# First layer of a fused transformer kernel: split float32r products against plain float32 products, and GpSimd's arithmetic moved to VectorE

## The chip, the cores and the metric

The kernel runs on one core of one Trainium2 chip. A core has the engines TensorE (PE; its weight loads are PEld), VectorE (DVE), ScalarE (ACT), GpSimd (POOL) and SyncE (SP), which here only issues DMAs. The metric is device time in microseconds (us) of one execution; smaller is better.

## The reference, cut to what matters

A sequence of 256 tokens of width 1024 goes through two transformer layers and then through a further block with experts. Only the first layer's mixing part ("even" layer) is touched. It computes, in float32:

```
hn = rmsnorm(x);  q, k, v, u = split(hn @ even_w_in)          # 1024 -> 512+128+128+512
o_attn = local attention with sinks (8 query heads, 2 key heads, window 128)
lam = exp(dt * a);  h_t = lam * h_{t-1} + (w*b) u_t            # complex state, 32 groups x 64
y = Re(c h) + d*u;  y = gelu(y);  o_ssm = y * sigmoid(y @ w_glu + b_glu)
x = x + concat(o_attn, o_ssm) @ even_w_out                     # 1024 -> 1024
```

What follows (a feed-forward part, an attention layer, another feed-forward part, a mixer with two kinds of attention, a memory layer, 32 experts) is not touched.

## The kernel before, in words

The program is written as Python that emits instructions into tiles. A list scheduler decides each engine's order at build time, from dependencies, program order and a model of costs; `after(...)` adds an order by hand on one engine. Each engine then runs its own list in order.

A **split product** stores a float32 matrix as two float32r tiles: `put_split` (L181, L182) lets ScalarE write the rounded high part (`Copy`) and VectorE, or GpSimd where `self.low` says so, write the low part by a subtraction. `mm3` then makes three matmuls, high by high, high by low and low by high. All products with weights in the kernel are of this kind. A plain float32 product is one `matmul` in the code; the trace shows it as two PE records.

`even()` runs in this order of the program:

- `x` and the first weights are loaded. `Norm.part` turns x by 16 transposes; VectorE multiplies by the gain (L1714) and the halves are split (`exh`, `exl`).
- The product for u: 4 outputs of 128 rows by 8 slices of 128, 256 columns each (`gemm_ws`). Then q, k, v: 3 pieces of 256 columns by 2 halves of the tokens by 8 slices (`gemm_ts`). Each piece of weights of 1 MB is loaded by SP into one of three buffers (`wrot`), then split into `hrot`.
- `S5.scalars` computes the state-space factors, some 90 small VectorE instructions (powers by `cmul`, L1841 to L1843). `inputs` (L1926, L1938) writes the input factors into `bd`, `rotations` (L1966 to L1970) builds a table by doubling. `outputs` (L2010, L2012, L2017, L2022) computes the output factors Q on GpSimd.
- `inputs_T` transposes bd (PE group s5F), `direct` multiplies bd by Q (PE group s5K), ScalarE copies the result to KT in pieces of 32 partitions, and GpSimd adds the diagonal (L2045).
- `qk_norm` and `swa`: two blocks of attention; scores (sc), a masked maximum on VectorE (L616), exponentials on ScalarE, the transposed weights (pTp), the product with v (swo), then a split into `mixa`.
- `step(j)`, four times: VectorE turns the inputs by the table, runs the recurrence as a scan (L2084) and turns back; PE makes y from KT, Q and the states.
- `gate`: gelu, a reshuffle (yt), a split, the product with `ssm_w_glu` (glu: 4 outputs by 4 slices, 256 columns), sigmoid, product, a split into `mixb`.
- `out_proj`: 8 slices by 2 halves of the tokens by 2 halves of the columns, 512 columns each (acc); the half on `mixa` can run before `gate` is done. GpSimd makes the low parts of four slices of `even_w_out` and of `ssm_w_glu`.

Buffers: `wrot` has 3 and `hrot` 4 buffers of 8 KB per partition; the pool `rot` (`r8`) has 4 more for u, the two bd, tables, attention, steps and the gate.

Of the kernel before, what the change touches and what calls it, by code (L numbers as in the profile page):

```python
# [44 lines left out]
class K:  # L45
# [269 lines left out]
    def accumulate(self, acc, pieces, t, first, last, cs=(0, 1)):  # L315

        ts = slice(t * P, (t + 1) * P)
        k = [(lhs[f], wp[f]) for lhs, wp in pieces for f in range(len(lhs))]
        for c in cs:
            cols = slice(c * 512, (c + 1) * 512)  # L320
            for i, ((lh, ll), (wh, wl)) in enumerate(k):
                self.mm3(acc[t][c], (lh[:, ts], ll[:, ts]), (wh[:, 0, cols], wl[:, 0, cols]),
                         first and i == 0, last and i == len(k) - 1)
# [43 lines left out]
    def even(self, x):  # L367
        nc, a = self.nc, self.a
        ctx = ExitStack()
# [8 lines left out]
        ectx = ExitStack()  # L378
        s5.ff = self.pool("s5F", 1, ectx, side="right")
# [18 lines left out]
        gotten = nc.vector.tensor_copy(gc, pg[:, 0:8]).ins  # L398
# [3 lines left out]
        nrm = Norm(self, x, None, "ex")  # L402
        nrm.gc = gc, s5.work().rearrange("p (k n) -> p k n", k=8)
        xp = nrm.xp
        tw, order = [], []
        for c in range(2):
            with self.after(*order):
                for t in range(2):
                    nrm.part(t, c)
            if c == 0:  # L410
                with self.after(*self.hold):
                    tw.append(self.split(tu[0][:, :, 0:P]))
                order = self.last
        sub = self.hold[1]
        with self.after(order[1]):
            s5.scalars()
        with self.after(self.turned):
            self.warm(warm, 6)
        for j, t in enumerate(tu):
            for f in range(1 - j, 2):  # L420
                self.low = nc.gpsimd if len(tw) == 1 else None
                tw.append(self.split(t[:, :, f * P:(f + 1) * P]))
        self.hold = []
        after = self.last[0]
        uT = self.r8("uT")[:, 0:1024].rearrange("p (t b a) -> p t b a", t=4, b=4)
        pu = [self.ps("u") for _ in range(2)]
        for j in range(2):
            for f in range(2):
                self.gemm_ws(pu[j][:, f * S:(f + 1) * S], tw[2 * j + f], xp)
            if j == 0:  # L430
                with self.after(self.lastmm, self.last[0]):
                    s5.factors()

        qk = ep.tile([P, 2, 10, 64], F32)
        v = ep.tile([P, 2, P], F32)
        pq = []
        for j in range(3):
            pq.append(self.ps("qkv"))
            self.gemm_ts(pq[j], self.wcolk(w, j * 256), xp)
            if j == 0:  # L440
                with self.after(sub):
                    r, R = nrm.both()
                for i in range(2):
                    for f in range(2):
                        nc.vector.tensor_tensor(uT[:, 2 * i + f],
                                                pu[i][:, f * S:(f + 1) * S].rearrange("p (a b) -> p b a", b=4),
                                                R.rearrange("p (a b) -> p b a", b=4), op=OP.mult)
            pv = pq[j].rearrange("p (t h d) -> p t h d", t=2, d=64)
            for t in range(2):
                if j < 2:  # L450
                    nc.scalar.activation(qk[:, t, 4 * j:4 * j + 4], pv[:, t], AF.Copy, scale=r[:, t:t + 1])
                else:
                    nc.scalar.activation(qk[:, t, 8:10], pv[:, t, 0:2], AF.Copy, scale=r[:, t:t + 1])
                    nc.scalar.activation(v[:, t], pq[j][:, t * 256 + P:t * 256 + 256], AF.Copy, scale=r[:, t:t + 1])

        qg = ep.tile([P, 2, 2, 64], F32)
        for i, n in enumerate(("q_norm", "k_norm")):
# [4 lines left out]
        nc.sync.dma_start(bglu, a["ssm_b_glu"][0].rearrange("(t p) -> p t", p=P))  # L462
        s5.outputs()
        s5.inputs(after)
        sink8 = ep.tile([P, 8], F32)
        nc.vector.tensor_scalar(sink8.rearrange("p (g h) -> p g h", g=2),
                                sink.rearrange("p (h g) -> p g h", g=2), 8.0, None, op0=OP.mult)
# [3 lines left out]
        nc.gpsimd.tensor_tensor(qg[:, 0], qg[:, 0], qg[:, 1], op=OP.mult)  # L471
        rq = ep.tile([P, 2, 8], F32)
        heads = self.qk_norm(ap, qk, qg[:, 0], qT, kT, rq)
        next(heads)
        s5.shuffle(uT)
        s5.inputs_T()
# [7 lines left out]
        mixa = self.r8("mixa", F32R).rearrange("p (c k n) -> p c k n", c=2, k=4)  # L484
        swa = [self.swa(ap, t, qT, kT, v, sink8, rq[:, t], mixa) for t in range(2)]
        s5.rotations(range(3))
        s5.direct()
        with self.after(s5.mark):
            next(heads, None)
        with self.after(self.normed):  # L490
            s5.rotations(range(3, 6))
        s5.decays()
# [3 lines left out]
        for j in range(4):  # L496
            s5.step(j)
            if j < 2:
                next(swa[j], None)
                mixed = self.last[0]  # L500
            if j == 2:
                ectx.close()
                hp = self.pool("s5g", 1, ctx, side="right")
                mid = [hp.tile([P, 2048], F32R, name=f"wh{i}") for i in range(2)]
        fctx.close()
        hp = self.pool("s5h", 1, ctx)
        mixb = hp.tile([P, 2, 4, S], F32R, name="mixb")
        mid += [hp.tile([P, 2048], F32R, name=f"wh{i}") for i in range(2, 4)]
        self.low, self.hold = nc.gpsimd, [s5.done]
        s5.gate(bglu, mixb)  # L510
        pctx.close()
        keep = self.hrot
        self.xgbuf = s5.work
        b = self.hrot[-1]
        self.hrot, self.nh = [b] * 2 + [lambda m=m: m for m in mid] + [lambda: self.r8("wh", F32R)] * 2, -1
        wo = a["even_w_out"][0]


        def pieces(j):
            self.low = nc.gpsimd if j < 2 else None  # L520
            if j == 1:
                self.hold = [mixed]
            if j >= 2:
                return self.wrows(wo, j * 256)
            wt = self.wtile(2, D)
            for gq in range(2):
                src = bass.AP(tensor=wo.tensor, offset=wo.offset + (gq * 256 + j * 64) * D,
                              ap=[[D, 64], [128 * D, 2], [1, D]])
                nc.sync.dma_start(wt[64 * gq:64 * gq + 64], src)
            return [self.split(wt[:, f:f + 1]) for f in range(2)]  # L530

        self.out_proj(x, pieces, [(m[:, 0, k], m[:, 1, k]) for m in (mixa, mixb) for k in range(4)])
        self.hrot, self.low = keep, None
        ctx.close()

    def r8(self, name, dt=F32):
        return self.rot.tile([P, 2048], dt, tag="r8", name=name)

    def qk_norm(self, pool, qk, qg, qT, kT, rq):
# [12 lines left out]
        for t in range(2):  # L552
            kt = qk[:, t, 8:10]
            nc.vector.tensor_tensor(kt, kt, r[:, t, 8:10, None].to_broadcast([P, 2, 64]), op=OP.mult)
            self.normed = nc.vector.tensor_tensor(kt, kt, qg, op=OP.mult).ins
        nc.vector.tensor_copy(rq.rearrange("p t (g h) -> p t g h", g=2),
                              r[:, :, 0:8].rearrange("p t (h g) -> p t g h", g=2))
        yield
# [14 lines left out]
    def swa(self, pool, t, qT, kT, v, sink8, rq, mix):  # L573
# [18 lines left out]
        self.last = self.put_split(mix[:, 0, :, ts], mix[:, 1, :, ts], o.rearrange("p (k n) -> p k n", k=4))  # L592
# [1092 lines left out]
class Norm:  # L1685
# [3 lines left out]
    def __init__(self, k, x, g_row, name, xp=None, g=None, pool=None):  # L1689
# [5 lines left out]
        self.gc = None  # L1695

    def part(self, t, c):
# [13 lines left out]
        if self.gc:  # L1711

            gc, tmp = self.gc
            k.nc.vector.tensor_tensor(tmp[sl], pv, gc[:, sl[1], None].to_broadcast([P, 4, P]), op=OP.mult)  # L1714
            pv = tmp[sl]
# [63 lines left out]
class S5:  # L1779
# [19 lines left out]
    def zeros(self):  # L1799
# [4 lines left out]
        self.bd = [k.r8(f"bd{c}").rearrange("p (s b q) -> p s b q", s=16, b=4) for c in range(2)]  # L1804
# [3 lines left out]
    def load_b(self):  # L1808
        nc, a = self.nc, self.k.a
        self.bn = self.r0[:, 1024:1536].rearrange("p (c s q) -> p c s q", c=2, s=16)  # L1810
        for c, n in enumerate(("ssm_b_re", "ssm_b_im")):
            nc.sync.dma_start(self.bn[:, c], bass.AP(tensor=a[n].tensor, offset=a[n].offset,
                                                     ap=[[16, P], [2048, 16], [1, 16]]))
# [12 lines left out]
    def work(self):  # L1826
        return self.sp.tile([P, 2048], F32, tag="ub", name="ub")
# [86 lines left out]
    def inputs(self, after):  # L1914

        nc, k, bn = self.nc, self.k, self.bn
        V, G = nc.vector, nc.gpsimd
        bd = self.bd
        bn = bn.rearrange("p c (t j) q -> p c j t q", j=4)
        u1, u2 = [self.ub[:, i * 512:(i + 1) * 512].rearrange("p (c s q) -> p c s q", c=2, s=16) for i in range(2)]  # L1920
        for b in (3, 2, 1, 0):
            p = 3 - b
            if p:
                for u, c in ((u1, 0), (u2, 1)):
                    for i in range(2):
                        V.tensor_tensor(u[:, i].rearrange("p (j t) q -> p j t q", j=4), bn[:, c],  # L1926
                                        self.lam[p][:, c + i].rearrange("p (j t) -> p j t", j=4)[:, :, :, None]
                                        .to_broadcast([P, 4, 4, 16]), op=OP.mult)
            for g in range(2):
                pr = slice(64 * g, 64 * g + 64)  # L1930
                qs = slice(16 * g, 16 * g + 16)
                for c in range(2):
                    if p == 0:
                        with k.after(after):
                            nc.scalar.activation(bd[c].rearrange("p (j t) b q -> p j t b q", j=4)[pr, :, :, b, qs],
                                                 bn[pr, c], AF.Copy)
# [227 lines left out]
```

## Time and profile before

| | us |
|---|---|
| median of 3 runs (lowest, highest) | 1379.64 (1378.18, 1383.82) |
| the profiled execution's own time | 1385.1 |
| its span, first to last instruction | 1383.2 |
| PE busy | 1254.5 (91%) |
| PEld / DVE / ACT / POOL busy | 941.7 / 677.3 / 500.7 / 101.3 |
| granted TensorE clock, mean | 0.958 |

The span runs from the first to the last instruction of the profiled execution; 1.9 us of its time lie around it. Busy is the time in which an engine has an instruction under way. [...] The first layer's mixing part takes the first 172 us.

### The profile page before, as it was taken

How to read it: one execution, taken by the hardware profiler on the slowest of the kernel's cores; microseconds unless marked ns; L12 is line 12 of the kernel's file. 1: busy time of each engine (PE TensorE's matmuls, PEld its weight loads, DVE VectorE, ACT ScalarE, POOL GpSimd, SP SyncE). 2: the span in 40 equal slices, each digit the busy share in tenths (PEclk: the TensorE clock that was granted, in tenths of full speed). 3: DMA queues.
4: the chain of work that ended last, by engine and by line, in shares of the span. 5: the costliest groups of instructions: out<-in, count | busy, mean ns of one | idle time of the engine just before them, and what ended most of it. 6: DMA issues, size and time to landing. Idle time of an engine off the chain costs nothing.

```text
span 1383.2 us, 20505 instructions
## 1 busy us (share of the span) xinstructions
PE 1254.5 (91%) x8559; PEld 941.7 (68%) x8559; DVE 677.3 (49%) x1139; ACT 500.7 (36%) x801; POOL 101.3 (7%) x101
## 2 busy tenths in 40 slices
PE   8589999999999999999999999999788777888786
PEld 7487899999999899999999998974222222122211
DVE  8986676566758776656865577731000000000001
ACT  5263564444558564444555555540000000000002
POOL 5641200000100000000400000000000000000000
PEclk9896899999999999999999999999999998999998
DMA  8211386553434585554265548789999999999996
GB/s 240 61 63 46 109 300 211 190 187 131 151 100 153 193 278 188 190 172 146 81 193 168 181 174 275 269 325 393 421 421 421 421 422 421 421 421 421 421 386 233
DMA packets 147309, 345.81 MB, mean 250 GB/s; under 512 B 13863, under 2 KB 104063, under 8 KB 124174
## 3 DMA queue, kind: packets, MB, share of 16 engines
q1 hardware_dynamic: 145546, 339.66, 66.3%
q0 software_dynamic: 1632, 4.80, 1.1%
q8 instruction: 68, 1.11, 0.3%
q14 instruction: 27, 0.22, 0.0%
q10 hardware_dynamic: 36, 0.01, 0.0%
HBM read 343.38 MB, written 1.06 MB: 249 GB/s over the span
## 4 chain that ended last, share of the span: by engine, by line
PE 60%; DMA 30%; DVE 6%; ACT 2%; issue 1%; POOL 0%; SPq 0%; DVEq 0%; ACTq 0%
PE gu L77 19%; PE acc L77 14%; DMA w<-in_w_exp_up_dram 10%; DMA w<-in_w_exp_gate_dram 9%; DMA w<-in_w_exp_down_dram 8%; PE z L77 4%; PE qk L77 3%; PE y L77 2%; PE v L77 2%; PE mqk L77 2%; PE prj L77 2%; DMA b<-in_w_exp_gate_dram 1%; DMA b<-in_w_exp_up_dram 1%; PE psT L1708 1%; PE mv L77 1%; PE cq L77 1%
## 5 line engine op out<-in xcount | busy, mean ns | idle before, releaser
L182 DVE TENSOR_TENSOR wh<-w,wh 128x1024 fp32r<-128x1024 f32 x242 | 293.3, 1230 | 143.5 <-ACT wh L181 143.2
L181 ACT ACTIVATE wh<-w 128x1024 fp32r<-128x1024 f32 x249 | 257.1, 1054 | 222.5 <-PE gu L77 61.2
L77 PE MATMUL gu<-fxh,wh 128*128 128x256 f32 x1408 | 257.5, 283 | 0.0
L77 PE MATMUL gu<-w,xe 128*32 128x512 f32 x920 | 178.6, 674 | 49.6 <-DMA w<-in_w_exp_gate_dram 27.2
L77 PEld LDWEIGHTS gu<-fxh,wh 128*128 128x128 f32 x1408 | 221.0, 192 | 0.8
L77 PE MATMUL gu<-fxl,wh 128*128 128x256 f32 x704 | 199.2, 283 | 0.0
L77 PEld LDWEIGHTS gu<-w,xe 128*32 128x32 f32 x920 | 39.2, 121 | 169.3 <-issue 69.7
L77 PEld LDWEIGHTS gu<-fxl,wh 128*128 128x128 f32 x704 | 135.0, 192 | 0.8
L77 PE MATMUL y<-w,hT 128*32 128x512 f32 x456 | 103.8, 613 | 18.6 <-DMA w<-in_w_exp_down_dram 13.1
L77 PE MATMUL acc<-wh,hh 128*128 128x512 f32 x352 | 109.3, 392 | 0.0
L77 PEld LDWEIGHTS y<-w,hT 128*32 128x32 f32 x456 | 24.8, 110 | 89.9 <-DMA w<-in_w_exp_down_dram 42.9
L77 PEld LDWEIGHTS acc<-wh,hh 128*128 128x128 f32 x352 | 64.5, 188 | 12.1
L1408 DVE COPY ot<-owT 128x256 f32<-128x256 f32 x8 | 3.4, 425 | 138.9 <-PE owT L1406 138.9
L77 PE MATMUL acc<-wh,hl 128*128 128x512 f32 x176 | 68.5, 389 | 0.0
L1450 DVE TENSOR_TENSOR y<-y,gu 128x512 f32<-128x512 f32 x8 | 8.1, 1013 | 110.2 <-PE gu L77 100.3
L1447 ACT ACTIVATE y<-gu 128x512 f32<-128x512 f32 x8 | 4.8, 597 | 152.4 <-PE gu L77 152.4
L1481 DVE COPY y<-y 128x512 f32<-128x512 f32 x7 | 4.8, 691 | 105.9 <-PE y L77 105.9
L1467 ACT ACTIVATE hT<-hT 128x512 f32<-128x512 f32 x8 | 4.8, 597 | 136.6 <-PE hT L1465 136.6
L77 PE MATMUL qk<-oxh,wh 128*128 128x256 f32 x256 | 49.7, 288 | 0.0
L77 PE MATMUL z<-mxh,wh 128*128 128x256 f32 x256 | 48.5, 286 | 0.0
L1479 ACT ACTIVATE y<-y 128x512 f32<-128x512 f32 x9 | 5.4, 597 | 115.4 <-PE y L77 115.4
L77 PE MATMUL gu<-b,xe 128*32 128x512 f32 x104 | 37.3, 665 | 7.4 <-DMA b<-in_w_exp_gate_dram 4.5
(535 smaller groups left out, 2177.7 us busy)
## 6 DMA issues: line engine op xcount, KB each, us to landing
w<-in_w_exp_gate_dram SPq DMA_DIRECT2D x57, 1024.0 KB, 19.8
w<-in_w_exp_up_dram SPq DMA_DIRECT2D x54, 1024.0 KB, 19.8
w<-in_w_exp_down_dram SPq DMA_DIRECT2D x51, 1024.0 KB, 19.8
w<-in_ffn_w_gate_dram SPq DMA_DIRECT2D x22, 1024.0 KB, 5.4
w<-in_ffn_w_up_dram SPq DMA_DIRECT2D x22, 1024.0 KB, 6.8
w<-in_ffn_w_down_dram SPq DMA_DIRECT2D x22, 1024.0 KB, 5.1
w<-in_w_in_dram SPq DMA_DIRECT2D x20, 1024.0 KB, 5.7
w<-in_odd_w_in_dram SPq DMA_DIRECT2D x12, 1024.0 KB, 6.4
```

The source lines that it names most:

```text
L77: self.lastmm = self.nc.tensor.matmul(out, lhsT, rhs, start=start, stop=stop, **kw).ins
L181: return (self.nc.scalar.activation(h, src, AF.Copy).ins, (eng or self.nc.vector).tensor_tensor(l, src, h.bitcast(F32), op=OP.subtract).ins)
L182: (eng or self.nc.vector).tensor_tensor(l, src, h.bitcast(F32), op=OP.subtract).ins)
L1408: V.tensor_copy(ot, ps[:, 0:256].rearrange("p (t n) -> p t n", t=2))
L1447: nc.scalar.activation(s, hs[0], AF.Silu)
L1450: V.tensor_tensor(sk, s.rearrange(turn, k=4), hs[1].rearrange(turn, k=4), op=OP.mult)
L1467: nc.scalar.activation(hT, ps.rearrange("p (f n) -> p f n", f=4), AF.Copy)
L1479: nc.scalar.activation(y[:, h], yps[h], AF.Copy)
L1481: V.tensor_copy(y[:, h], yps[h])
L1708: k.turned = k.nc.tensor.transpose(ps[:, i * P:(i + 1) * P], xg[:, t, (4 * c + i) * P:(4 * c + i + 1) * P], k.ident).ins
```

## The change

Of the first layer's mixing part only:

- All split products become plain float32 products: u, q/k/v, glu, out_proj. Weights are used as they are loaded, and the splits of weights and activations go (those of q/k/v's input, of y, mixa and mixb too).
- x is turned in another order (two slices by both halves of the tokens per PSUM tile). The gain is multiplied in by VectorE for half of the tiles and by ScalarE's scale for the other half.
- The two bd move from `rot` to two of the `hrot` buffers, and the two weight tiles of u to the other two. The q/k/v weights take the three `wrot` buffers at once. `even_w_out`'s first two pieces and `ssm_w_glu` follow in `wrot`; its last two pieces go into `rot` buffers, loaded in the program after `gate`.
- `outputs` runs on VectorE. The diagonal is no longer added: ScalarE writes 16 scaled identities into KT (free from the start), and `direct` adds them by 16 more matmuls of 128 columns; KT is then copied in 4 pieces of 128 partitions.
- b is loaded by 8 DMAs on GpSimd's queue in place of 2 on SP's.
- In program order `shuffle`, `inputs_T`, all rotations and decays come before `outputs` and `qk_norm`; some hand-made orders go. GpSimd keeps memsets, masks and DMAs.

```diff
@@ gemm_ws, accumulate (alike)
+            if not isinstance(wp, tuple):
+                self.mm(out, wp[:, k, fs], xp[:, k], first and k == 0, k == nk - 1)
+                continue
@@ even
+        h = self.hrot[0]
+        s5.bd = [h().bitcast(F32).rearrange("p (s b q) -> p s b q", s=16, b=4) for c in range(2)]
+        self.wrot, self.nw = [lambda: h().bitcast(F32)] * 2 + self.wbase, -1
...
-                tw.append(self.split(t[:, :, f * P:(f + 1) * P]))
...
-                self.gemm_ws(pu[j][:, f * S:(f + 1) * S], tw[2 * j + f], xp)
+                self.gemm_ws(pu[j][:, f * S:(f + 1) * S], tu[j], xT, f=f)
...
+        r, R = nrm.both()
+        s5.inputs()
...
-            self.gemm_ts(pq[j], self.wcolk(w, j * 256), xp)
+            wt = self.load_cols(w, j * 256)
+            for t in range(2):
+                for k in range(8):
+                    self.mm(pq[:, t * 256:(t + 1) * 256], xT[:, k, t * P:(t + 1) * P], wt[:, k], k == 0, k == 7)
...
+        self.wrot, self.nw = self.wbase, -1
+        wos = [heads_rows(0)]
+        wglu = self.load(a["ssm_w_glu"][0].rearrange("(k p) n -> p k n", p=P))
+        wos.append(heads_rows(1))
+        s5.shuffle(uT)
+        s5.inputs_T()
+        s5.rotations(range(6))
+        s5.decays()
         s5.outputs()
...
+        self.hold = [s5.gate(wglu, bglu, mixb)]
+        for j in range(2, 4):
+            wt = self.r8("wo").rearrange("p (a b) -> p a b", a=2)
+            nc.sync.dma_start(wt, wo[j * 256:(j + 1) * 256, :].rearrange("(k p) n -> p k n", p=P))
+            wos.append(wt)
@@ load_b
-            nc.sync.dma_start(self.bn[:, c], bass.AP(tensor=a[n].tensor, offset=a[n].offset,
+            for j in range(4):
+                nc.gpsimd.dma_start(self.bn[:, c, 4 * j:4 * j + 4],
@@ outputs
-            G.tensor_tensor(v1, cd[:, 0:1].to_broadcast(shp), self.pw[i][:, 1:3, :, None].to_broadcast(shp),
+            V.tensor_tensor(v1, cd[:, 0:1].to_broadcast(shp), self.pw[i][:, 1:3, :, None].to_broadcast(shp),
...
-                self.done = G.tensor_tensor(Q[pr, :, :, i, qs], v1[pr], v2[pr], op=OP.add).ins
+                V.tensor_tensor(Q[pr, :, :, i, qs], v1[pr], v2[pr], op=OP.add)
@@ direct
+                k.mm(ps[:, i * P:(i + 1) * P], k.ident, KT[:, s].rearrange("p b q -> p (b q)"), True, False,
+                     skip_group_check=True)
...
-            self.done = nc.gpsimd.tensor_tensor(KT[pr, :, b], KT[pr, :, b], self.dI[pr], op=OP.add).ins
+            nc.scalar.activation(KT[:, 4 * s4:4 * s4 + 4], pk, AF.Copy)
```

## Rows read from the trace of the kernel before

**Rows 1.** Page, part 2: busy tenths of the span in 40 slices of 34.6 us

```profile
PE   8589999999999999999999999999788777888786
DVE  8986676566758776656865577731000000000001
POOL 5641200000100000000400000000000000000000
PEclk9896899999999999999999999999999998999998
```

**Rows 2.** Windows by stage: busy us (instructions) of PE, PEld, DVE, ACT, POOL; clock; DMA

```profile
5.30:83.20 77.90, 55.21 (x613) 50.83 (x611) 75.28 (x178) 38.08 (x72) 39.23 (x31) 0.87 0.47 120
101.30:172.20 70.90, 67.92 (x343) 55.19 (x344) 44.21 (x63) 31.16 (x57) 14.59 (x12) 0.77 0.25 80
172.00:1383.00 1211.00, 1113.14 (x7478) 818.65 (x7476) 539.53 (x845) 419.79 (x642) 28.17 (x43) 0.97 0.72 271
```

**Rows 3.** Timeline: first and last of 27 stretched VectorE rows, and their neighbours

```profile
13.10 0.19 DVE L1886 TENSOR_TENSOR t<-pr 128x32 f32<-128x32 f32 x1
...
13.25 2.38 POOL L182 TENSOR_TENSOR wh<-w,wh 128x1024 fp32r<-128x1024 f32 x1 [5.50 <-ACT wh L181]
...
13.32 2.33 DVE L1887 TENSOR_TENSOR den<-t 128x16 f32<-128x16 f32 x1
...
68.14 2.16 DVE L1938 TENSOR_TENSOR bd<-ub 64x256 f32<-64x256 f32 x3
```

**Rows 4.** Prices of VectorE's rows that go and come, undisturbed; groups and timeline

```profile
16.46 1.23 DVE L182 TENSOR_TENSOR wh<-w,wh 128x1024 fp32r<-128x1024 f32 x1
...
L182 DVE TENSOR_TENSOR exl<-ub,exh 128x512 fp32r<-128x512 f32 x4 | 2.6, 687 | 0.7 <-ACT exh L181 0.7
L1714 DVE TENSOR_TENSOR ub<-psT,gc 128x512 f32<-128x512 f32 x4 | 2.6, 683 | 0.2 <-PE psT L1708 0.2
...
77.53 0.69 DVE L1966 TENSOR_TENSOR tb<-T,E 128x512 f32<-128x512 f32 x1
```

**Rows 5.** Timeline: one DMA issue on GpSimd's queue

```profile
131.94 0.74 POOL L212 DMA_DIRECT2D gain<-in_ffn_norm_dram  x1 [5.63 <-DVE abgh L2084]
```

**Rows 6.** Prices of matmuls: three pieces of the chain, then groups by shape

```profile
75.18 7.11 PE s5K L77 x144
...
158.51 9.55 PE acc L77 x42
...
174.65 9.83 PE gu L77 x82
...
L77 PE MATMUL sc<-kT,qT 128*128 128x256 f32 x16 | 3.6, 379 | 0.0
...
L77 PE MATMUL acc<-y,ot 128*128 128x512 f32 x64 | 29.9, 607 | 1.4 <-ACT y L1479 1.4
```

**Rows 7.** Waits of PE in 0 to 172 us

```profile
PE qkv L77 <- DVE wh L182: 14.0, 2, 11.2
PE pTp L77 <- DVE dgp L649: 3.9, 1, 3.9
PE yt L77 <- DVE abgh L2077: 2.9, 1, 2.9
```

**Rows 8.** Timeline: where the stages begin and end

```profile
9.15 0.39 PE L77 MATMUL u<-exh,wh 128*128 128x256 f32 x1 [0.34 <-ACT wh L181]
...
86.47 0.29 DVE L616 CUSTOM_DVE_ANT_0 att<-sc,band 128x128 f32<-128x128 f32 x1 [3.27 <-PE sc L77]
...
101.32 3.33 PE L77 MATMUL pTp<-dgp,att 128*128 128x128 f32 x14 [3.89 <-DVE dgp L649]
...
170.04 2.31 PE L77 MATMUL acc<-wh,mixb 128*128 128x512 f32 x9
```

**Rows 9.** One window of 4 us, columns as in rows 2

```profile
144.00:148.00 4.00, 4.00 (x24) 1.83 (x25) 2.36 (x2) 2.81 (x4) 0.00 (x0) 0.50 0.00 0
```

**Rows 10.** DMA view, 0 to 200 us: issues, KB each, median us to landing

```profile
w<-in_even_w_out_dram SPq DMA_DIRECT2D x2, 1024.0 KB, 5.1
```

More of the change, by code (lines that the diff above doesn't have):

```diff
@@ L320, in accumulate @@
             cols = slice(c * 512, (c + 1) * 512)
-            for i, ((lh, ll), (wh, wl)) in enumerate(k):
+            for i, (l, w) in enumerate(k):
+                if not isinstance(w, tuple):
+                    self.mm(acc[t][c], l[:, ts], w[:, 0, cols], first and i == 0, last and i == len(k) - 1)
+                    continue
+                (lh, ll), (wh, wl) = l, w
                 self.mm3(acc[t][c], (lh[:, ts], ll[:, ts]), (wh[:, 0, cols], wl[:, 0, cols]),
@@ L401, in even @@
         s5.load_rest()
[L402 to L415, printed above, removed]
-            s5.scalars()
[L417 to L421, printed above, removed]
-                tw.append(self.split(t[:, :, f * P:(f + 1) * P]))
-        self.hold = []
-        after = self.last[0]
+        nrm = Norm(self, x, None, "ex", xp=())
+        xT = self.xpool.tile([P, 8, S], F32, tag="xTl", name="ex")
+        for j in range(4):
+            ps = self.ps("psT")
+            for i in range(4):
+                k = 2 * j + i // 2
+                nc.tensor.transpose(ps[:, i * P:(i + 1) * P], x[:, i % 2, k * P:(k + 1) * P], self.ident)
+            pv = ps.rearrange("p (k n) -> p k n", k=2)
+            ks = slice(2 * j, 2 * j + 2)
+            if j % 2 == 0:
+                turned = V.tensor_tensor(xT[:, ks], pv, gc[:, ks, None].to_broadcast([P, 2, S]), op=OP.mult).ins
+            else:
+                for i in range(2):
+                    nc.scalar.activation(xT[:, 2 * j + i], pv[:, i], AF.Copy, scale=gc[:, 2 * j + i:2 * j + i + 1])
+        with self.after(turned):
+            s5.scalars()
+        self.warm(warm, 4)
         uT = self.r8("uT")[:, 0:1024].rearrange("p (t b a) -> p t b a", t=4, b=4)
@@ L462, in even, with heads_rows @@
         nc.sync.dma_start(bglu, a["ssm_b_glu"][0].rearrange("(t p) -> p t", p=P))
+        wo = a["even_w_out"][0]
+        def heads_rows(j):
+            wt = self.wtile(2, D)
+            for gq in range(2):
+                src = bass.AP(tensor=wo.tensor, offset=wo.offset + (gq * 256 + j * 64) * D,
+                              ap=[[D, 64], [128 * D, 2], [1, D]])
+                nc.sync.dma_start(wt[64 * gq:64 * gq + 64], src)
+            return wt
+        self.wrot, self.nw = self.wbase, -1
[6 more added lines that the diff above has]
+        s5.decays()
         s5.outputs()
-        s5.inputs(after)
         sink8 = ep.tile([P, 8], F32)
-        nc.vector.tensor_scalar(sink8.rearrange("p (g h) -> p g h", g=2),
-                                sink.rearrange("p (h g) -> p g h", g=2), 8.0, None, op0=OP.mult)
+        V.tensor_scalar(sink8.rearrange("p (g h) -> p g h", g=2),
+                        sink.rearrange("p (h g) -> p g h", g=2), 8.0, None, op0=OP.mult)
         qT = ep.tile([P, 4, S], F32)
@@ L483, in even @@
                                 fill=NEG, base=-1, channel_multiplier=-1)
-        mixa = self.r8("mixa", F32R).rearrange("p (c k n) -> p c k n", c=2, k=4)
+        mixa = ep.tile([P, 4, S], F32, name="mixa")
         swa = [self.swa(ap, t, qT, kT, v, sink8, rq[:, t], mixa) for t in range(2)]
-        s5.rotations(range(3))
         s5.direct()
[L488 to L492, printed above, removed]
         next(swa[0])
@@ L499, in even, with r8 @@
                 next(swa[j], None)
[L500 to L504, printed above, removed]
-        fctx.close()
[L506 to L510, printed above, removed]
-        pctx.close()
[L512 to L533, printed above, removed]
+        fctx.close()
+        pctx.close()
+        mixb = self.r8("mixb")[:, 0:1024].rearrange("p (k n) -> p k n", k=4)
+        self.hold = [s5.gate(wglu, bglu, mixb)]
[3 more added lines that the diff above has]
+            wos.append(wt)
+        self.xgbuf = lambda: self.r8("xg")
+        self.wrot = keep
+        self.out_proj(x, lambda j: [wos[j][:, f:f + 1] for f in range(2)], [m[:, k] for m in (mixa, mixb) for k in range(4)])
         ctx.close()
-    def r8(self, name, dt=F32):
-        return self.rot.tile([P, 2048], dt, tag="r8", name=name)
+    def r8(self, name):
+        return self.rot.tile([P, 2048], F32, tag="r8", name=name)
     def qk_norm(self, pool, qk, qg, qT, kT, rq):
@@ L2016, in outputs @@
                 qs = slice(16 * g, 16 * g + 16)
-                self.done = G.tensor_tensor(Q[pr, :, :, i, qs], v1[pr], v2[pr], op=OP.add).ins
-            order.close()
-        self.dI = dI = sp.tile([P, 16, 32], F32, name="dI")
-        for b in range(4):
-            pr = slice(32 * b, 32 * b + 32)
-            G.tensor_tensor(dI[pr], k.ident[pr, None, pr].to_broadcast([32, 16, 32]),
-                            d2[pr, :, None].to_broadcast([32, 16, 32]), op=OP.mult)
+                V.tensor_tensor(Q[pr, :, :, i, qs], v1[pr], v2[pr], op=OP.add)
     def direct(self):
```

134 lines of the change are left out of this document (54 added, 80 removed).

## The prediction

> **What bounds the kernel now.** The page's tenths come first: TensorE is busy nearly throughout, except in the first four or five slices, where VectorE is full, GpSimd works, and the granted clock dips to a mean of 0.6 in one slice [rows 1]. So only there can an edit of other engines give time. The windows by stage say it in numbers: from 5.3 to 83.2 us VectorE is busy 75.28 of 77.90 us, TensorE only 55.21; from 101.3 to 172.2 us TensorE is busy 67.92 of 70.90 us at a mean clock of 0.77; the 1211.0 us behind them are TensorE's at 0.97, later the weight DMAs' of the experts [rows 2]. What the first part loses or gains is carried on whole: later weight loads go out when buffers come free, so they move with it.
>
> VectorE's 75 us are not all work. A multiplication of 128x32 takes 0.19 us; the next small one, begun 0.07 us after GpSimd began a subtraction of 2.38 us, takes 2.33 us and ends with it; the last of 27 such rows is a 64x256 addition, three in 2.16 us [rows 3]. For these 27 I took each one's time less that of the same shape away from GpSimd: 26.3 us in all. TensorE waits for this engine: 14.0 us before q/k/v, 3.9 us before pTp, 2.9 us before yt [rows 7]. The reader should see a stage bound by VectorE up to 83.2 us (86.47 less the 3.27 us it then waits for the scores) [rows 8], and then one bound by TensorE, partly at half clock.
>
> **Stage A, to the first maximum of the scores (86.47 us).** VectorE's list before ended at 83.2 us.
> - The stretching goes with GpSimd's two-input work: −26.3 us. GpSimd's busy time of 39.23 us is the most that it can be [rows 2]; nothing excludes less if other waits lie under it, so 0 is the other end. I take 26.3, since it is counted row by row.
> - Splits go: 9 of 128x1024 by 1.23 us = 11.1; the four low parts of x, 2.6; half of the four gain products, 1.3 [rows 4]. Together −15.0 us.
> - `outputs` comes: 5 rounds of 2 products of 128x512 and 2 sums of 64x512. The nearest row is a 128x512 product of `rotations`, 0.69 us [rows 4]; the 64-partition sums have as many elements per partition. 20 by 0.69 = +13.8 us.
> VectorE's list then ends near 83.2 − 26.3 − 15.0 + 13.8 = 55.7 us.
>
> TensorE now gets close. A split product of 256 columns is three matmuls of 9.83/82 = 0.12 us: 0.36. A plain one is two records: 3.6/16 by 2 = 0.45 us. For 512 columns it is 3 by 9.55/42 = 0.68 against 2 by 29.9/64 = 0.93 [rows 6]. The first u product starts at 9.15 us [rows 8]; 32 for u and 48 for q/k/v by 0.45 take 36.0 us, to 45.2; s5F, which ran from 70.3 to 75.18 us [rows 3, 6], takes 4.9, to 50.1 us. Then `direct` needs the first four rounds of Q: if VectorE does the last round (4 by 0.69 = 2.8 us) behind them, at 52.9 us. It costs 7.11 us as before plus 16 matmuls of 128 columns at half of 0.45: 3.6 us [rows 6], to 63.6 us. From there to the first maximum it was 4.2 us (82.29 to 86.47) [rows 6, 8]. So 67.8 us: **18.7 us earlier**. VectorE would have given more; TensorE's added work takes part of it. At nothing I cost: ScalarE's 16 scaled identities and its eviction of half of x (it is busy 38.08 of 77.90 us [rows 2], and KT is free from the start); GpSimd's diagonal, which leaves the path to y. The 8 loads of b cost GpSimd's queue 8 by 0.74 = 5.9 us [rows 5], behind memsets that are over early; VectorE's scalars cover them. If that cover fails, `inputs` is late by that much. SP's queue is two issues shorter in front of the q/k/v weights, which now have a buffer each and wait for no split.
>
> **Stage B, to pTp (101.32 us).** It lasted 14.85 us, of which TensorE waited 3.9 for VectorE [rows 7, 8], while GpSimd split pieces of `even_w_out`. Without that the work of TensorE in front should be the limit: 10.95 us, so 78.8 us, **22.6 us earlier**. Bounds: 0 to 3.9 us of this wait stay; I take 0, since the same wait's engine is freed.
>
> **Stage C, to the last `even_w_out` matmul (170.04 + 2.31 = 172.35 us).** It is TensorE's stage: 67.92 us busy at 0.77 [rows 2] is 52.3 us of work at full clock. The change adds 16 by 0.09 = 1.4 us (glu) and 32 by 0.25 = 8.0 us (out_proj) [rows 6]: 61.7 us. The splits of y, mixa, mixb and the weights that go lay under TensorE and give nothing; their cover is this same busy engine. The open price is the clock. At 1.00 the stage takes 61.7 us, at the old 0.77 it takes 80.1, and between 0 and 3.0 us of idle come on top. The clock's low slice stands behind the two waits of 3.9 and 2.9 us [rows 1, 7], and both hang on VectorE; but a window in which TensorE is busy all of its 4.00 us still shows 0.50 [rows 9], so full work alone did not bring it back there. I take the middle, 0.885, and 2 us of idle: 71.7 us, to 150.5 us.
>
> [...]
>
> **Sum.** 172.35 − 150.5 = 21.9 us less. Against the profiled execution that is 1385.1 − 21.9 = 1363.2 us; that execution lay 5.5 us above the median of the runs, so I forecast 1379.6 − 21.9 = **1357.7 us**. Measurements of this kernel tell about 0.5% (6.9 us) from no change.
>
> **Rivals.**
> - *Full clock.* No wait is long enough to lose the clock in stage C: 61.7 us, to 140.5 us, 31.9 us less: 1347.8 us. With `direct` starting at 50.1 instead of 52.9, 1345. For it: the waits hang on VectorE. Against: rows 9. [...]
> - *Old clock and late weights.* 0.77 and 3.0 us of idle: 83.1 us, to 161.9 us, 10.5 us less: 1369.2 us. The last piece of `even_w_out` needs a `rot` buffer, and mixb and two tiles of the gate hold three of four, so its load may go out only when the gate ends; such a load takes 5.1 us to land [rows 10]. Other products cover some of it. Uncovered: 1374.3 us.
> - *No change.* As the last, and the 3.9 us before pTp stay: 1.4 us less, 1378.2 us. So it would be if VectorE's stretched rows hide waits on chains of small dependent instructions, so that the 26.3 us are not work to be had.
> [...]
> - *Not what it says.* If the list scheduler puts `outputs` or `direct` late, TensorE idles before `direct`; this ends between the second and the third.
>
> **Chances.** Forecast 0.45, full clock 0.22, old clock or late weights 0.17, no change 0.08, slower 0.08. So faster by over 0.5%: 0.84, within: 0.08, slower: 0.08. The range goes from the full-clock case with a little more (1343) to the late weights (1374) and leaves out the last two cases, 0.16.
>
> **What would show it.** In the changed profile: VectorE's rows of 128x16 to 128x48 all near 0.2 us, and no two-input row on GpSimd; the wait of q/k/v for VectorE gone; first maximum near 68 us, pTp near 79, last `even_w_out` matmul near 150; plain products at 0.45 and 0.93 us. Wrong if the first maximum comes after 75 us (stage A's sum), if plain products cost over 0.6 us, if the clock in stage C is under 0.77, or if the time behind the last `even_w_out` matmul differs from 1211 us by more than 3.

## The result, and the profile after

The changed kernel took 1362.91 us (median of 4 runs, 1362.80 to 1363.17) against 1381.73 us of the kernel before (4 runs, 1378.18 to 1385.18): ratio 0.987, 95% interval 0.984 to 0.990. Run again later it took 1362.21 against 1377.62 us: ratio 0.989 (0.987 to 0.990). It is faster by some 1.2%, and inside the predicted range; the point forecast of 1357.7 was 5.2 us too low. The profiled execution took 1362.8 us, span 1361.1.

Two of the page's rows of tenths for the changed kernel, over 40 slices of 34.0 us, answer to [rows 1]: GpSimd is nearly empty, and the clock's low slice among the first five has gone (9899 and then 9, where it was 9896 and 8).

```profile
POOL 4010000000100000000400000000000000000000
PEclk9899999999999999999999999999898798898889
```

Where the stages of the changed kernel begin and end, in its timelines of VectorE and TensorE; the rows answer to [rows 8]:

```profile
78.12 0.29 DVE L608 CUSTOM_DVE_ANT_0 att<-sc,band 128x128 f32<-128x128 f32 x1 [17.72 <-PE sc L77]
...
89.46 0.78 PE L77 MATMUL pTp<-dgp,att 128*128 128x128 f32 x5
...
97.38 2.94 PE L77 MATMUL pTp<-dgp,att 128*128 128x128 f32 x24 [1.26 <-DVE dgp L641]
...
148.62 2.74 PE L77 MATMUL acc<-wo,mixb 128*128 128x512 f32 x6
```

| end of, us | before | forecast | after |
|---|---|---|---|
| stage A, first maximum | 86.47 | 67.8 | 78.12 |
| stage B, first pTp | 101.32 | 78.8 | 89.46 |
| stage C, last `even_w_out` matmul | 172.35 | 150.5 | 151.36 |
| from there to the end of the span | 1210.9 | 1211 | 1209.7 |

So the end of the layer was forecast to 0.9 us, but by two errors that happen to cancel: stage A ends 10.3 us later than forecast, and stage C is 9.8 us shorter (61.9 us where 71.7 were taken). The windows of those two stages, columns as in [rows 2], say how. VectorE's list up to the first maximum now ends at 60.4 us, 22.8 earlier, though VectorE is still busy 51.44 of 55.10 us up to there; TensorE is busy 49.22 of them and goes on alone from there. In stage C TensorE runs at a granted clock of 1.00 where it had 0.77 (1.00 is full speed).

```profile
5.30:60.40 55.10, 49.22 (x308) 41.45 (x308) 51.44 (x178) 23.40 (x61) 9.38 (x12) 0.97 0.68 169
...
89.40:151.40 62.00, 60.16 (x299) 37.94 (x298) 31.54 (x48) 22.73 (x46) 6.14 (x11) 1.00 0.53 169
```

What TensorE waits for in the first 152 us: the 14.0, 3.9 and 2.9 us of [rows 7] are gone, and a new wait for the keys stands first. The 1.3 us for pTp are not what is left of the 3.9: those stood before the first pTp, at the end of stage B, and TensorE is now busy in all of stage B; the 1.3 us stand before the second block's pTp at 97.38 us, in stage C.

```profile
PE kT L77 <- DVE qk L548: 4.1, 1, 4.1
PE pTp L77 <- DVE dgp L641: 1.3, 1, 1.3
```

That wait lies in the midst of `direct`. In TensorE's timeline s5K has begun; then the transposes of q and k, which the list scheduler put among its matmuls, wait 4.05 us for VectorE. Later the two rows of each of the 16 steps follow one another every 0.97 us: 0.42 for the identity product, 0.55 for the rest.

```profile
55.42 0.49 PE L77 MATMUL s5K<-KT,ident 128*128 128x128 f32 x2
59.96 1.12 PE L77 MATMUL kT<-ident,qk 128*64 128x128 f32 x8 [4.05 <-DVE qk L548]
...
72.36 0.62 PE L77 MATMUL s5K<-Q,wh 128*32 128x128 f32 x16
72.91 0.49 PE L77 MATMUL s5K<-KT,ident 128*128 128x128 f32 x2
73.33 0.62 PE L77 MATMUL s5K<-Q,wh 128*32 128x128 f32 x16
```

The windows of 4 us around the wait, columns as in [rows 2]: 0.04 us of TensorE's work, then full work at a clock of 0.50.

```profile
56.00:60.00 4.00, 0.04 (x2) 0.04 (x2) 3.61 (x18) 0.00 (x0) 0.00 (x0) 0.68 0.01 2
60.00:64.00 4.00, 4.00 (x36) 2.73 (x36) 0.36 (x3) 2.10 (x5) 0.00 (x0) 0.50 0.01 4
```

Plain products cost what was forecast or less. A row of TensorE's timeline has 48 products of 256 columns, two records each, in 20.88 us: 0.435 each.

```profile
26.04 20.88 PE L77 MATMUL qkv<-w,ex 128*128 128x256 f32 x96
```

Two pieces of the chain: 16 products of 256 columns in 6.93 us are 0.433 each, 24 of 512 columns in 20.60 us 0.858.

```profile
119.03 6.93 PE glu L77 x32
125.96 20.60 PE acc L77 x48
```

### The profile page after: what moved, and what is told of

It reads as the page before. It is cut to its first block, busy times and chain, and to the rows that moved or that the text cites. A ratio compares the mean times of both kernels' runs of the same rounds, so it can differ in the third digit from the quotient of the medians.

```text
span 1361.1 us, 20234 instructions
## 1 busy us (share of the span) xinstructions
PE 1258.8 (92%) x8459; PEld 927.2 (68%) x8459; DVE 636.3 (47%) x1124; ACT 479.5 (35%) x780; POOL 46.8 (3%) x72
## 3 DMA queue, kind: packets, MB, share of 16 engines
HBM read 343.38 MB, written 1.06 MB: 253 GB/s over the span
## 4 chain that ended last, share of the span: by engine, by line
PE 60%; DMA 31%; DVE 5%; ACT 2%; issue 1%; SPq 0%; DVEq 0%; ACTq 0%
PE gu L77 19%; PE acc L77 15%; DMA w<-in_w_exp_gate_dram 10%; DMA w<-in_w_exp_down_dram 10%; DMA w<-in_w_exp_up_dram 9%; PE z L77 4%; PE qk L77 3%; PE v L77 2%; PE mqk L77 2%; PE prj L77 2%; DMA b<-in_w_exp_up_dram 1%; PE psT L1699 1%; PE s5K L77 1%; PE mv L77 1%; PE y L77 1%; PE cq L77 1%
## 5 line engine op out<-in xcount | busy, mean ns | idle before, releaser
L182 DVE TENSOR_TENSOR wh<-w,wh 128x1024 fp32r<-128x1024 f32 x229 | 275.6, 1222 | 139.2 <-ACT wh L181 138.8
L181 ACT ACTIVATE wh<-w 128x1024 fp32r<-128x1024 f32 x229 | 236.6, 1054 | 203.3 <-PE gu L77 66.4
L77 PE MATMUL gu<-w,xe 128*32 128x512 f32 x920 | 183.0, 693 | 49.7 <-DMA w<-in_w_exp_gate_dram 28.0
L77 PE MATMUL y<-w,hT 128*32 128x512 f32 x456 | 100.7, 621 | 14.5 <-DMA w<-in_w_exp_down_dram 9.0
L77 PE MATMUL gu<-b,xe 128*32 128x512 f32 x104 | 41.6, 733 | 6.8 <-DMA b<-in_w_exp_gate_dram 4.6
```

The lines of the kernel that those rows point to most:

```text
L77: self.lastmm = self.nc.tensor.matmul(out, lhsT, rhs, start=start, stop=stop, **kw).ins
L181: return (self.nc.scalar.activation(h, src, AF.Copy).ins, (eng or self.nc.vector).tensor_tensor(l, src, h.bitcast(F32), op=OP.subtract).ins)
L182: (eng or self.nc.vector).tensor_tensor(l, src, h.bitcast(F32), op=OP.subtract).ins)
```

## The experiments

**Is it GpSimd or the plain products?** The kernel before keeps its split products, and GpSimd's two-input arithmetic moves to VectorE: all of it, the output factors alone, or the late splits alone. Orders made by hand for GpSimd's work go with it.

```diff
 outputs                                   (first and second kernel)
-        G = nc.gpsimd
+        G = nc.vector
 even, pieces                              (first and third kernel)
-        self.low, self.hold = nc.gpsimd, [s5.done]
+        self.low, self.hold = None, []
-            self.low = nc.gpsimd if j < 2 else None
+            self.low = None
 even, direct                              (first kernel)
-                self.low = nc.gpsimd if len(tw) == 1 else None
+                self.low = None
-            self.done = nc.gpsimd.tensor_tensor(KT[pr, :, b], KT[pr, :, b], self.dI[pr], op=OP.add).ins
+            self.done = nc.vector.tensor_tensor(KT[pr, :, b], KT[pr, :, b], self.dI[pr], op=OP.add).ins
```

> The kernel before, its split products kept, with every two-input operation that GpSimd does in the first layer moved to VectorE (the output factors, the scaled identities and their four additions, the splits of the weights, the gain product). Theory A (the gain is GpSimd's: its two-input work stretches VectorE's rows and so makes TensorE wait, after which the granted clock reads 0.50): VectorE's list of the first stage is 26 us shorter by the stretching and about 14 us longer by the output factors, so the first maximum comes at about 75 instead of 86.5 us; the 5.58 us pair of scans at 121.28 shrinks to about 1.3 us, the hole in TensorE at 124 to 128 goes and with it the twenty microseconds at 0.50; time 1355 to 1364 us, as short as the changed kernel or shorter. Theory B (the gain is that of the plain products, which need no splits): VectorE still makes every split and now GpSimd's too; the time stays within 5 us of the kernel before, 1376 us or more.

Measured: 1363.27 us, ratio 0.988 (0.985 to 0.991): as fast as the changed kernel, with every split product kept. Its timelines:

```profile
82.69 0.28 DVE L614 CUSTOM_DVE_ANT_0 att<-sc,band 128x128 f32<-128x128 f32 x1
...
92.95 2.02 PE L77 MATMUL pTp<-dgp,att 128*128 128x128 f32 x16
...
148.80 2.31 PE L77 MATMUL acc<-wh,mixb 128*128 128x512 f32 x9
```

The layer ends at 151.11 us, the changed kernel's at 151.36. Theory B has fallen. But the first maximum was expected at about 75 us: it comes 3.8 us earlier than before and no more, since VectorE, which now makes the splits and the four diagonal additions too, works right up to it. Most of the gain lies behind it: 4.6 us in stage B (10.3 for 14.85) and 12.9 in stage C (58.2 for 71.0). The rest of the change, taken together, gives nothing: it brings the first maximum 4.6 us forward (82.69 to 78.12), and gives that back by 1.1 us in stage B (10.3 to 11.3) and 3.7 in stage C (58.2 to 61.9).

> The kernel before with the output factors (20 operations on GpSimd and the four scaled-identity ones) on VectorE and nothing else changed; the late splits and the four additions stay on GpSimd. Theory A: first maximum 10 to 13 us earlier (about 75 us); stages behind it unchanged, the scans at 5.58 us and the 0.50 spells included; time 1366 to 1372 us. Theory B: VectorE gains 14 us of work, so nothing or up to 10 us slower.

Measured: 1371.04 us, ratio 0.994 (0.992 to 0.996). First maximum at 79.87 us, 6.6 earlier where 10 to 13 were expected; the 5.57 us pair of scans is still there, and so is the slow spell behind the wait of 2.91 us that follows it: four y records take 1.06 us, where they take 0.61 before it. The profile is of an execution of 1378.46 us, 7.4 above the median, so it compares with the profile of before, not with the medians. The layer's end, 6.4 us earlier than there:

```profile
163.59 2.31 PE L77 MATMUL acc<-wh,mixb 128*128 128x512 f32 x9
```

> The kernel before with only the late splits (gate weight and the first pieces of the output weight) on VectorE instead of GpSimd. Theory A: first stage as before (first maximum at 86.5 us); the scans beside the splits take 0.6 us each instead of 2.8, TensorE's hole at 124 to 128 us is under 1.5 us and the clock of 128 to 148 stays near 1.00, so that the last product of the layer ends 8 to 13 us earlier, less up to 3 us for the splits that VectorE now does: 1366 to 1374 us. Rival C (the half clock belongs to the narrow products of this stretch, whatever waits stand in it): the spell at 0.50 stays and the time is within 3 us of before.

Measured: 1370.66 us, ratio 0.994 (0.993 to 0.996). First maximum at 89.32 us, 2.9 later; but the pair of scans takes 1.27 us, the window in which the kernel before had its hole is full, and the layer ends at 158.85 us, 13.5 earlier than in the profile of before.

```profile
120.23 1.27 DVE L2082 TENSOR_TENSOR_SCAN abgh<-D,abgh 128x256 f32<-128x256 f32 x2
...
156.54 2.31 PE L77 MATMUL acc<-wh,mixb 128*128 128x512 f32 x9
```

Its window at the place of the hole (the next four, to 144 us, are full at 1.00 too):

```profile
124.00:128.00 4.00, 4.00 (x34) 3.42 (x29) 3.93 (x9) 0.00 (x0) 0.74 (x1) 1.00 0.00 0
```

The same narrow y products stand there, so rival C has fallen for this spell: with the hole, the half clock goes. The two parts add up: medians of −7.0 and −7.4 us beside −14.8 for all of it. But 13.5 us in the profiles against 7.4 in the medians asks for the next run.

**An execution of the kernel before near its median**, unchanged.

> The kernel before once more, for a profile of an execution near its median (the profile shown lay 5.5 us above it; executions of this kernel spread over 10 us, those of the changed kernel over 1 us). Theory F (the spread is the length of the half-clock spell behind the hole at 124 to 128 us): an execution of 1376 to 1379 us has the same hole and the same first maximum within 1 us, but a spell at 0.50 of 6 to 14 us instead of some 20, and its last product of the layer ends 5 to 8 us earlier, at 164 to 167 us; the time behind it stays within 1.5 us of 1211. Rival G (the spread arises behind the layer): the last product ends at 171 to 173 us, and the part behind it is 5 to 8 us shorter.

Measured: 1379.84 us for the profiled execution. First maximum 86.65 us, as before; the hole is there; then the spell at 0.50 lasts some 10 us, not 20, with TensorE full in both, as the windows show:

```profile
124.00:128.00 4.00, 1.41 (x8) 0.52 (x6) 4.00 (x3) 0.44 (x1) 2.61 (x1) 1.00 0.07 8
128.00:132.00 4.00, 3.67 (x13) 2.48 (x13) 3.97 (x9) 0.00 (x0) 0.00 (x0) 0.50 0.78 254
132.00:136.00 4.00, 4.00 (x21) 4.00 (x20) 1.95 (x3) 0.00 (x0) 0.75 (x1) 0.50 0.34 131
136.00:140.00 4.00, 4.00 (x20) 3.49 (x21) 0.00 (x0) 0.69 (x1) 0.00 (x0) 0.72 0.00 0
```

The last product, in TensorE's timeline:

```profile
165.58 2.32 PE L77 MATMUL acc<-wh,mixb 128*128 128x512 f32 x9
```

The layer ends at 167.90 us, 4.45 earlier than in the other profile (a little under the 5 to 8 expected), and 1210.2 us follow. Rival G has fallen: nearly all of the 5.3 us between the two executions lies in this spell. So the profile on which the prediction rests showed an execution with a long one. An earlier spell at 0.50, behind the 3.9 us before pTp, ends near 114 us in both.

**One part undone**: the output factors of the changed kernel back on GpSimd, with a scratch tile of their own.

```diff
 outputs
-        V = nc.vector
+        V = nc.gpsimd
+        vv = k.r8("vv")
...
-        v1, v2 = [self.ub[:, i * 512:(i + 1) * 512]...
+        v1, v2 = [vv[:, i * 512:(i + 1) * 512]...
```

> The changed kernel with one part undone: the products and sums of the output factors (20 operations) back on GpSimd, the scaled identities still on ScalarE. Theory A (GpSimd's two-input work stretches VectorE's rows, and what waits for VectorE comes late): VectorE rows beside it read about 1 to 2 us again instead of 0.2 to 0.7, VectorE's list ends at 65 to 75 us instead of 60.4 although it has 14 us less to do, and the time is 4 to 15 us over the changed kernel's, 1367 to 1378 us. Theory B (the move to VectorE brought nothing by itself): VectorE's list is 14 us shorter, TensorE no longer waits 4.05 us for the keys, and the time is 1356 to 1360 us.

Measured: 1372.17 us, ratio to before 0.995 (0.994 to 0.997), 9.3 us over the changed kernel (against the kernel before measured beside each, this one gains 5.7 us and the changed kernel 15.4). VectorE's list ends at 67.75 us, 7.3 later, with 13.8 us less to do. Its row of 128x48, 0.21 us in the changed kernel, lasts as long as GpSimd's beside it, and TensorE's last piece of q/k/v stands still. The profile names no releaser; by the program the piece needs the PSUM buffer of the first half of u, and VectorE's second of four rows that read u ends at 51.87 us, 0.1 before TensorE goes on:

```profile
34.55 1.10 DVE L1828 TENSOR_TENSOR cm<-l,l 128x48 f32<-128x48 f32 x1
...
34.52 1.06 POOL L1993 TENSOR_TENSOR vv<-cd,pw 128x512 f32<-128x512 f32 x1
...
51.97 9.35 PE L77 MATMUL qkv<-w,ex 128*128 128x256 f32 x32 [11.55 <-issue]
```

**One cost added**: nine idle operations on GpSimd in the changed kernel, beside the scans.

```diff
 even
+        s5.z = ep.tile([P, 512], F32, name="z")
 step
+        if j == 2:
+            z = Gs.rearrange("p c s -> p (c s)")
+            for _ in range(9):
+                nc.gpsimd.tensor_tensor(self.z, z, z, op=OP.subtract)
+                z = self.z
```

> The changed kernel with nine idle subtractions (128x512) added on GpSimd beside the scans of the third step of the state-space mixer; the first reads the scan's input, the rest only their own scratch tile, and nothing reads the result. No order on TensorE or VectorE differs. Theory A (two-input GpSimd work stretches VectorE's rows, TensorE then waits, and the clock falls behind the wait): the scan and the rows behind it take 1 to 2.5 us instead of 0.4 to 1.2, VectorE's last row of the mixer ends 7 to 10 us later than 109.1, TensorE has a hole of 4 to 9 us there, windows behind it read 0.50, and the time is 1370 to 1380 us. Rival C (the clock and the waits of this stretch have other causes): rows and clock as before, 1361 to 1365 us.

> The changed kernel itself once more, beside the next two on one chip, so that their distances don't rest on runs of another chip: 1361 to 1364 us, first maximum at 78 us, no granted clock under 1.00 between 68 and 152 us.

Measured on one chip: 1370.91 against 1362.21 us, 8.7 us slower (ratios to before 0.995, 0.994 to 0.997, and 0.989). The changed kernel itself came out as expected; the profile after, shown above, has the first maximum at 78.12 us and 1.00 in every window of 4 us from 68 to 152 us. In the kernel with the idle operations, first the timelines of VectorE and TensorE:

```profile
105.02 1.21 DVE L2048 TENSOR_TENSOR abgh<-v,T 128x1024 f32<-128x1024 f32 x1
106.15 1.24 DVE L2062 TENSOR_TENSOR abgh<-abgh 128x256 f32<-128x256 f32 x1
...
115.53 0.43 PE L77 MATMUL y<-abgh,Q 128*128 128x63 f32 x2 [2.63 <-DVE abgh L2062]
```

Then the windows behind TensorE's wait:

```profile
116.00:120.00 4.00, 4.00 (x16) 3.11 (x15) 0.00 (x0) 0.00 (x0) 0.00 (x0) 0.52 0.25 98
120.00:124.00 4.00, 4.00 (x18) 2.27 (x19) 0.00 (x0) 0.60 (x1) 0.00 (x0) 0.50 0.27 60
124.00:128.00 4.00, 4.00 (x28) 1.63 (x20) 0.69 (x1) 0.60 (x1) 0.00 (x0) 0.70 0.49 202
```

VectorE's mixer ends 6.7 us late (115.8 instead of 109.1), a little under the 7 to 10 expected. TensorE's hole is only 2.63 us, less than the 4 to 9 expected, and 0.5 before it; but behind it the clock reads 0.50 for some 10 us of full work, by an estimate from the three windows 5 us lost (4 us by 0.48, 0.50 and 0.30). The layer ends at 160.16 us instead of 151.36. The direction that the removal showed holds the other way round too.

**What made stage A late.** Three kernels from the changed one: the transposes of q and k behind `direct`; no identity products (VectorE adds to the identities in KT instead); both.

```diff
 even                                      (first and third)
-        self.qk_norm(ap, qk, qg[:, 0], qT, kT, rq)
+        heads = self.qk_norm(ap, qk, qg[:, 0], qT, kT, rq)
+        next(heads)
...
         s5.direct()
+        with self.after(s5.mark):
+            next(heads, None)
 direct                                    (second and third)
-                k.mm(ps[:, i * P:(i + 1) * P], k.ident, KT[:, s].rearrange("p b q -> p (b q)"), True, False,
-                     skip_group_check=True)
...
-            nc.scalar.activation(KT[:, 4 * s4:4 * s4 + 4], pk, AF.Copy)
+            for b in range(4):
+                o = KT[32 * b:32 * b + 32, 4 * s4:4 * s4 + 4, b:4]
+                nc.vector.tensor_tensor(o, o, pk[32 * b:32 * b + 32, :, b:4], op=OP.add)
```

> The changed kernel with the transposes of queries and keys put behind the direct term's matmuls on TensorE (they stand in their midst, wait 4.05 us for VectorE's key products, and the granted clock reads 0.50 behind that wait). Theory D (this wait and the slow clock behind it are what made the first maximum late): the 4.05 us and some 2 to 4 us of half clock go, first maximum at 70 to 74 us instead of 78.1, time 1356 to 1360 us. Rival E (the direct term is late because its 16 identity products cost more than I took, and ScalarE's copies of queries and keys now come onto the path): first maximum 76 to 80 us and the time within 1.5 us of the changed kernel's 1362.9.

> The changed kernel without the 16 identity products that start each direct term: VectorE adds the direct term to the scaled identities in 16 additions of 32 partitions instead (0.2 to 0.7 us each), in the place of ScalarE's four copies. If an identity product costs the 0.42 to 0.53 us read from the changed kernel, TensorE has 7 to 8 us less to do in the direct term, and the first maximum comes at 70 to 72 us: 1355 to 1358 us. If they lie beside the wait for the keys or VectorE's additions take their place, the first maximum moves by under 3 us: 1360 to 1363 us.

> Both edits together: transposes of queries and keys behind the direct term, and no identity products. If the two costs are separate they add: first maximum at 64 to 68 us, last product of the layer at 138 to 142, time 1350 to 1354 us. If the one only hides the other (VectorE's list ends at 60.4 us in any case and the keys come after it), the first maximum is at 68 to 71 us and the time 1354 to 1357 us.

Measured: 1357.22, 1357.84 and 1354.05 us; ratios to before 0.985 (0.982 to 0.988), 0.985 (0.982 to 0.988) and 0.983 (0.980 to 0.986). The first maximum comes at 72.29, 73.00 and 67.85 us: 5.8, 5.1 and together 10.3 us earlier, so the two costs are nearly separate up to there (the second came a little later than the 70 to 72 us expected). In time they add less well: against the kernel before measured beside them the three gain 20.6, 20.0 and 23.8 us, the changed kernel 15.4. In the third TensorE waits 2.1 us for VectorE's maxima, and behind that wait 8 records of the scores, 256 columns each, take 3.08 us: 0.385 each, where 3.6/16 = 0.225 were taken [rows 6]. With the wait out of it, the window from 56 to 60 us is full at 1.00 in the first. In the third, s5K is one run; the rows are of its TensorE's and VectorE's timelines:

```profile
53.53 7.15 PE L77 MATMUL s5K<-Q,wh 128*32 128x128 f32 x256 [1.14 <-ACT F L1936]
...
61.88 5.95 DVE L2021 TENSOR_TENSOR KT<-KT,s5K 32x512 f32<-32x512 f32 x12
67.85 0.29 DVE L612 CUSTOM_DVE_ANT_0 att<-sc,band 128x128 f32<-128x128 f32 x1
```

**The additions out of the way**: twelve of the sixteen move behind the first maxima.

```diff
 even, from the version with both edits
...
+        with self.after(self.nmark):
+            s5.diag(range(1, 4))
...
```

> The version with both edits, and twelve of the sixteen additions to the scaled identities moved behind the first maxima (they stand before them on VectorE, 61.9 to 67.8 us, though nothing needs them until the first y product). First maximum at 64.5 to 65.5 us instead of 67.85, and if nothing else is on the path there, 1350 to 1352 us; if the additions now hold up the second half's maxima or the state products, 1353 to 1355 us.

Measured: 1353.88 us, ratio 0.983 (0.982 to 0.985), 8.3 us under the changed kernel on the same chip, and no measurable gain over the version above. The first maximum comes at 64.62 us as expected, but pTp at 79.57 us against 79.64. Among TensorE's waits one that was not there before stands first, on what follows the additions in VectorE's list:

```profile
PE v L77 <- DVE abgh L2063: 2.4, 1, 2.4
```

Behind it 16 records of pTp take 3.73 us, 0.233 each, where the 24 from 88.22 us on take 2.90, 0.121 each: what the earlier maximum gave, this wait and the slow products behind it took back.

## Why the prediction was right, and where steps of it missed

- **The time lies in the range, in part by luck.** That VectorE's stretched rows and TensorE's waits behind them go is what happened. But stage A ended 10.3 us late and stage C was 9.8 us short, and only their sum came out. By the prediction's own sign, "Wrong if the first maximum comes after 75 us (stage A's sum)", stage A's sum was wrong: 78.12 us. In stage C it was the full-clock rival, with a chance of 0.22, that had the right clock.
- **The mechanism of stage A held.** The stretched rows were work to be had: undoing one part brings such rows back and costs 9.3 us; taking only GpSimd's work away gives all of the gain, though most of it behind stage A. But VectorE's list ended at 60.4 us against 55.7 forecast: its busy time fell by 23.8 us where 26.3 + 15.0 − 13.8 = 27.5 were forecast, and it idles 1.0 us more. Some 2 of these 4.7 us are rows that still stretch (last section); the rest is not traced. The start of s5K did not suffer (52.70 us, forecast 52.9); the keys, the last products of that list, did.
- **"It costs 7.11 us as before plus 16 matmuls of 128 columns at half of 0.45: 3.6 us" failed.** Half the columns were to cost half: 0.225 us. An identity product costs 0.42 us, and the 16 narrow rows behind each take 0.55, where they take 7.15/16 = 0.45 without it. Other plain products of 128 columns do cost about half (12 of pTp, two records each, in 2.94 us: 0.245 each), so neither columns nor records explain it; why the two kinds of product are dear when they alternate is not shown. Without the identity products s5K takes 7.15 us, as I took it; with them 16 by 0.97 = 15.5, so 4.8 us more than the 10.7 forecast.
- **A wait that was not forecast**: the scheduler put the transposes of q and k into the midst of `direct`, where they wait 4.05 us for VectorE's late keys, the clock then reads 0.50, and the transposes themselves run in that spell. With the list as late (59.99 us), the other order alone removes the wait. With both costs put right the first maximum came at 67.85 us. That the forecast said 67.8 is chance: this kernel has no identity products, for which the forecast had 3.6 us, and twelve additions of VectorE, 5.95 us, stand right before its maximum. With the additions moved it is 64.62 us, and 67.8 − 3.6 = 64.2. The rival "not what it says" named TensorE's idling before `direct`; it came inside it.
- **Stage B** lasted 11.3 us against 10.95, all of it TensorE's work: the 3.9 us went, as forecast.
- **Stage C's work was nearly right, its clock was mis-sized.** TensorE was busy 60.16 us at 1.00; the work was put at 61.7, and 2 us of idle at about what came. "I take the middle, 0.885" cost 8.0 us (61.7/0.885 less 61.7). The old mean of 0.77 came from two spells at 0.50 (the windows of 4 us from 103 to 111 and from 132 to 148 us read 0.50), behind the waits of 3.9 and 2.9 us; with these waits both spells went. What ends such a spell is not shown: without the long waits the window from 89.4 to 151.4 us reads 1.00, while in the kernel before TensorE worked through all of those windows at 0.50.
- **The late weight of `even_w_out`** cost nothing: the last piece's load goes out at 127.15 us and takes 6.8 us (5.1 were taken), the products on mixa cover it, and the first product on mixb follows them at 136.10 without a gap.
- **"That execution lay 5.5 us above the median of the runs, so I forecast 1379.6 − 21.9" failed, and with the layer's end right by chance this is the 5.2 us of the point forecast.** Between profiled executions the change saved 1385.1 − 1362.8 = 22.3 us, 21.9 forecast. But the 5.5 us above the median were for the most part the longer half-clock spell, which the change removes too. Against the execution of 1379.84 us it saves 17.0. I subtracted the same microseconds twice.
- **The rest of the change is worth nothing measurable as it stands**: the kernel with split products and no two-input work on GpSimd takes 1363.27 us. What the plain products alone are worth is not shown. They spare VectorE the splits of stage A; in stage C they are 8.3 us more work for TensorE (60.16 us at 1.00 against 55.17 at 0.94), where 1.4 + 8.0 were forecast. With the two costs of stage A gone, the plain kernel reaches 1354.05 us; a split kernel was not tuned in the same way.

## What to carry to other kernels

Two-input work on GpSimd was not free for VectorE here: beside a GpSimd product of 1.06 us a VectorE row of 0.21 us took 1.10, and the 20 operations of the output factors on GpSimd cost 9.3 us. Look for small VectorE rows that last exactly as long as a GpSimd row beside them, and count what waits for VectorE before calling GpSimd's busy time cheap. A hole in TensorE cost more behind it than in it (one of 2.63 us was followed by some 10 us of full work at 0.50, an estimated 5 us lost), so a wait is to be priced with the clock of the windows that follow. A total that comes out right is to be checked stage by stage: here two errors of 10 us cancelled. And where the profiled execution lies off the median, ask first whether the excess is part of what the change removes.

## What the runs showed of the hardware that was not expected

- The half-clock spell behind a hole has no fixed length though TensorE is full in it: some 20 and 10 us in two executions of one kernel behind the same hole, some 12 us in both behind the 3.9 us before pTp, 10 us behind a hole of 2.63 us, and some 4 us of work behind the 4.05 us before the keys. What sets it stays open. That the spread of the kernel before (1375.9 to 1386.3 us in 15 runs) is this spell, where the changed kernel's 4 runs lie within 0.4 us, is shown for two executions and only argued for the rest. The version with both edits, though in its profile the slow products behind the 2.1 us wait are soon over (32 records of v take 4.30 us, the next 32 3.74), spreads from 1352.95 to 1361.06 us in 6 runs.
- Beside GpSimd's rows only some of VectorE's stretch: in the kernel with the nine idle operations, a row with one operand in PSUM (`v`) and one in SBUF of 128x1024 takes 1.21 us, as it does without them in the changed kernel (1.22), and the next, of 128x256 with both in SBUF, 1.24 instead of 0.42. The row before them, of 128x1024 like the first but with both in SBUF, takes 1.88 instead of 1.22. How far this reaches beyond these rows is not shown.
- Not only two-input work on GpSimd stretches rows: the prediction's sign "VectorE's rows of 128x16 to 128x48 all near 0.2 us" failed for a few. In the changed kernel a row of 128x16 with one input takes 1.20 us instead of 0.17 beside two memsets of GpSimd that end at 13.44 us, and one of 128x2 at 9.28 us takes 1.47 beside GpSimd's DMA issues, where it takes 0.16 in the kernel before; together they hold VectorE up by an estimated 2 us (1.20 − 0.17 and 1.47 − 0.16). No run takes these memsets or issues away, so the cause is read from the times alone.

```profile
12.27 1.20 DVE L1857 TENSOR_SCALAR kk<-kk 128x16 f32<-128x16 f32 x1
...
12.22 0.97 POOL L495 MEMSET kT<- 128x1024 f32 x1
```
